# Forget-gate products of the next head queued in equal shares behind the score levels, and merge-gate blocks spread over three heads

## The chip, the cores and the metric

The kernel runs on one core of a Trainium2 chip. The metric is the device time of one execution in microseconds (us), the median of several runs. In the rows, PE is the matrix engine (TensorE) and PEld its weight loads, DVE is VectorE, ACT is ScalarE, POOL is GpSimd, and SP issues the DMA transfers.

## The reference, cut to what matters

One encoder layer over 1024 positions and 1024 channels. A combined projection of the normalised input gives, among others, `q`, two forget gates (forward and backward), the values, and two merge gates. The part around the change is the bidirectional gated recurrence with eight heads of 128 channels, and the sigmoid of one merge gate:

```python
f = lb + (1.0 - lb) * sigmoid(zf)          # forget gate, per direction
k = (1.0 - lb) * sigmoid(-zf)
S_t = diag(f_t) S_{t-1} + k_t v_t^T        # per head, forward and backward
o_t = S_t^T q_t
merged = sigmoid(ga) * (A @ W_a) + sigmoid(gb) * (Bm @ W_b)
```

After it come an output projection, a gated feed-forward block and a per-layer embedding gate, which the change doesn't touch.

## The kernel before, in words

Everything is float32. Large products are done as three passes of a reduced type (high by high, high by low, low by high): `mm3` at line 127 issues, for each of eight blocks of 128 input channels, three products with 512 moving columns into one PSUM bank, so 24 products for a block of 128 output channels and 512 positions (all recorded at L133).

The kernel goes through stages: input norm and token-major projections, the other branch, the channel-major columns (lines 514 to 548), **the heads** (lines 551 to 774), merge, output projection, feed-forward and the last gate. The change lies in the stage of the heads alone.

For each head `h` the loop at line 759 does, in program order:

- `scores(h)` (line 601). VectorE builds `ks` (L607) and `QA` (L606) from the head's `q`, keys `X`, `Y` and forget gates `F`. TensorE makes the diagonal score products (L613), then seven levels (block sizes 1 to 64). A level has two halves `g` of four score products (L624; each float32 product is two instructions of 128 columns). Between levels VectorE multiplies `QA` (L633) and `X` (L636) by forget gates, ScalarE copies a part of `Y` (L657), GpSimd makes the next `Y` (L660), VectorE merges scores under a mask (L646; ScalarE at the two last levels, L643), and `F` is folded to half its length (L666). The next level reads the updated `QA` and `X`.
- `proj(nxt, h + 1, "qfbg")` (line 561): the forget gates of the next head, in both directions. Two weight blocks are loaded and split (L114 and L115 behind the load in `load_split`), and for each of two halves of the positions `mm3` runs: 4 x 24 = 96 products. ScalarE and VectorE then write `F`, `X` and `Y` of that head (L591 to L599). `F` has one buffer, so the next head's is written only after the first level of the current head has read the old one; the `mm` tag of PSUM has three banks.
- `outputs(h, cur)` (line 670): 14 transposes of the last `X` and `Y` (L683), copied by ScalarE (L685), 28 instructions of state products (L688), a chain of state updates on VectorE (L692, L694), 44 instructions of output products (L712), a norm (L715, L719) and a last transpose (L722, L724).

At the last head, which has no next head to project, `gate_a(0)` and `gate_a(1)` (lines 766 and 769) compute four blocks of the merge gate (`j` from 4 to 7) for one half of the positions each: 8 x 24 = 192 products, and each call loads and splits the four weight blocks anew. The four earlier blocks of this gate are made in the stage before. `hT` is freed after these products, and the two halves `A0` and `A1` of the attention output are loaded and split into its place for `merge` (line 785).

The order of the instructions on each engine isn't the program's: the framework schedules at compile time, on a simulated timeline; among the instructions whose inputs and buffers are ready it takes the one that comes first in the program. On the chip each engine keeps that order. Products of `proj` and `gate_a` are thus put wherever TensorE has, by that timeline, nothing earlier in the program that is ready, limited by free PSUM banks and by `F`.

Of the kernel before, what the change touches and what calls it, by code (L numbers as in the profile page):

```python
# [17 lines left out]
P = 128  # L18
# [3 lines left out]
KD = D // P  # L22
# [13 lines left out]
def kernel(ctx: ExitStack, tc: tile.TileContext, a: dict, out: bass.AP):  # L36
# [7 lines left out]
    nc = tc.nc  # L44
# [72 lines left out]
    def load_split(src, shape, eng, pool, rpool, tag="whl"):  # L117

        raw = rpool.tile([P] + shape, F32, name="raw", tag="raw")
        nc.sync.dma_start(raw, src)  # L120
        hl = pool.tile([P, 2] + shape, F32R, name="whl", tag=tag)
        split_into(hl[:, 0], hl[:, 1], raw, eng)
        return hl
# [3 lines left out]
    def mm3(ps, lhs, rhs, nk):  # L127

        n = nk * len(PASSES)
        i = 0  # L130
        for k in range(nk):
            for lp, rp in PASSES:
                nc.tensor.matmul(ps, lhsT=lhs(lp, k), rhs=rhs(rp, k), start=(i == 0), stop=(i == n - 1))  # L133
                i += 1
# [6 lines left out]
    def fm_rhs(fm):  # L141
        return lambda p, k: fm[p][k // 4][:, k % 4, :]
# [29 lines left out]
    class Seven:  # L172


        def __init__(self, w, raw, t, ev, zbanks):
            self.w, self.raw, self.t, self.ev, self.zbanks, self.n = w, raw, t, ev, zbanks, 0
            self.first, self.second = None, None
# [113 lines left out]
    c_raw, rawp = phase("raw", 2)  # L291
# [259 lines left out]
    c_hg, hg = phase("hg")  # L551
    c_t, t1 = phase("s1t", 2)

    class Head:
        pass

    def view(t, off, dims):
        tv = t[:]
        return bass.AP(tv.tensor, tv.offset + off, [list(tv.ap[0])] + dims)

    def proj(s, h, kinds):

        for kind in kinds:
            if kind == "q":
                s.q = hg.tile([P, T], F32, name="q", bufs=2)
                nc.sync.dma_start(s.q, q_d[h])  # L570
                continue
            if kind == "g":
                s.zg = hg.tile([P, T], F32, name="zg", bufs=2)
                nc.sync.dma_start(s.zg, zg_d[h])
                s.v = hg.tile([P, NT, P], F32, name="v", bufs=2)
                nc.sync.dma_start(s.v, v_d[h])
                continue
            if kind == "f":
                s.F = hg.tile([P, 2, T], F32, name="F")
                s.X = hg.tile([P, T], F32, name="X0", bufs=2)  # L580
                s.Y = hg.tile([P, T], F32, name="Y", bufs=2)
            w = load_split(a["w_fm"][{"f": 8, "b": 16}[kind] + h], [KD, P], None, whlp, rawp)
            for n in range(2):
                ns = slice(n * NH, (n + 1) * NH)
                ps = ps_tile("mm")
                mm3(ps, lambda p, k: w[:, p, k, :], fm_rhs(hT[n]), KD)
                d = 0 if kind == "f" else 1
                om = oml[:, d, h:h + 1]
                Fd = s.F[:, 1 - d, ns]
                sg = t2(t1, "sk")  # L590
                nc.scalar.activation(sg, ps, AF.Sigmoid, scale=-1.0)  # L591
                nc.scalar.activation(Fd, ps, AF.Sigmoid)
                sv = sg.rearrange("p (t h) -> p t h", h=2)
                for par in range(2):
                    dst = (s.X if par == d else s.Y).rearrange("p (t h) -> p t h", h=2)
                    nc.scalar.activation(dst[:, n * NH // 2:(n + 1) * NH // 2, par], sv[:, :, par],
                                         AF.Identity, scale=om)
                nc.scalar.activation(Fd, Fd, AF.Identity, scale=om, bias=lbt[:, d, h:h + 1])
                nc.vector.tensor_scalar(out=Fd, in0=Fd, scalar1=TINY, scalar2=None, op0=ALU.max)  # L599

    def scores(h, s):
        q, X, Y, F = s.q, s.X, s.Y, s.F
        QA = hg.tile([P, 2, T], F32, name="QA", bufs=2)
        ks = hg.tile([P, T], F32, name="ks")
        SC = hg.tile([P, NT, P], F32, name="SC", bufs=2)
        nc.vector.tensor_tensor(out=QA, in0=view(q, 0, [[0, 2], [1, T]]), in1=F, op=ALU.mult)  # L606
        nc.vector.tensor_tensor(out=ks, in0=X, in1=Y, op=ALU.add)  # L607

        for g in range(2):
            sp = ps_tile("sc")  # L610
            for i in range(4):
                cs = slice((4 * g + i) * P, (4 * g + i + 1) * P)
                nc.tensor.matmul(sp[:, i * P:(i + 1) * P], lhsT=ks[:, cs], rhs=q[:, cs], start=True, stop=True)  # L613
            nc.scalar.activation(SC[:, 4 * g:4 * g + 4], sp.rearrange("p (c t) -> p c t", c=4), AF.Copy)

        for li, m in enumerate(LEVELS):
            nb = T // m
            cb = P // (2 * m)

            def level(g):  # L620
                sp = ps_tile("sc")
                for i in range(4):
                    c = 4 * g + i
                    nc.tensor.matmul(  # L624
                        sp[:, i * P:(i + 1) * P], lhsT=X[:, c * P:(c + 1) * P],
                        rhs=view(QA, c * P, [[2 * m, cb], [T + m, 2], [1, m]]), start=True, stop=True)
                return sp

            def update(g, X2):

                o, of = g * NH, g * nb // 2
                qd = [[T + m, 2], [2 * m, nb // 4], [1, m]]
                nc.vector.tensor_tensor(out=view(QA, o, qd), in0=view(QA, o, qd),  # L633
                                        in1=view(F, of + 1, [[nb - 1, 2], [2, nb // 4], [0, m]]), op=ALU.mult)
                dims = [[4 * m, nb // 8], [3 * m, 2], [1, m]]
                nc.vector.tensor_tensor(out=view(X2, o, dims), in0=view(X, o, dims),  # L636
                                        in1=view(F, nb + of + 1, [[4, nb // 8], [1 - nb, 2], [0, m]]), op=ALU.mult)

            def merge(g, sp):
                if m >= 32:  # L640
                    for p0 in range(0, P, m):
                        c0 = p0 ^ m
                        nc.scalar.activation(SC[p0:p0 + m, 4 * g:4 * g + 4, c0:c0 + m],  # L643
                                             sp.rearrange("p (c t) -> p c t", c=4)[p0:p0 + m, :, c0:c0 + m], AF.Copy)
                    return
                nc.vector.copy_predicated(  # L646
                    SC[:, 4 * g:4 * g + 4], masks[:, li, None, :].broadcast_to([P, 4, P]),
                    sp.rearrange("p (c t) -> p c t", c=4))

            X2 = hg.tile([P, T], F32, name="X", bufs=3)  # L650
            sp0 = level(0)
            update(0, X2)
            merge(0, sp0)
            sp1 = level(1)

            mid = [[4 * m, nb // 4], [1, 2 * m]]
            nc.scalar.activation(view(X2, m, mid), view(Y, m, mid), AF.Copy)  # L657
            update(1, X2)
            mid = [[4 * m, nb // 4], [m, 2], [1, m]]
            nc.gpsimd.tensor_tensor(out=view(Y, m, mid), in0=view(X, m, mid),  # L660
                                    in1=view(F, 0, [[4, nb // 4], [nb + 3, 2], [0, m]]), op=ALU.mult)
            X = X2
            merge(1, sp1)
            F2 = hg.tile([P, 2, nb // 2], F32, name=f"F{2 * m}", bufs=2 if m == 64 else 1)
            Fv = F.rearrange("p d (b h) -> p d b h", h=2)
            nc.vector.tensor_tensor(out=F2, in0=Fv[:, :, :, 0], in1=Fv[:, :, :, 1], op=ALU.mult)  # L666
            F = F2
        s.QA, s.SC, s.X, s.Y, s.F = QA, SC, X, Y, F
# [76 lines left out]
        split_into(w[:, 0], w[:, 1], raw)  # L745
        return w

    def gate_a(n):
        for j in range(NGA, KD):
            w = load_split(a["w_fm"][24 + j], [KD, P], None, whlp, rawp)  # L750
            ps = ps_tile("mm")
            mm3(ps, lambda p, k: w[:, p, k, :], fm_rhs(hT[n]), KD)
            sg = t2(t1, "sk")
            nc.scalar.activation(sg, ps, AF.Sigmoid)
            nc.sync.dma_start(sig_d[j, :, n * NH:(n + 1) * NH], sg)

    cur = Head()
    proj(cur, 0, "qfbg")
    for h in range(H):
        nxt = Head()  # L760
        scores(h, cur)
        if h + 1 < H:
            proj(nxt, h + 1, "qfbg")
        if h == H - 1:

            gate_a(0)
            A0 = new_fm("A0")
            load_A(0, A0, range(H - 1), 5)
            gate_a(1)
            A1 = new_fm("A1")  # L770
            wa = [split_wa(load_wa(j)) for j in range(2)]
        outputs(h, cur)
        cur = nxt
# [320 lines left out]
```

## Time and profile before

| | |
|---|---|
| three runs | 1965.67, 1969.12, 1968.33 us, median 1968.33 us |
| the profiled execution | 1966.99 us, with a span of 1965.2 us from the first to the last instruction |
| TensorE | 97% of the span busy, granted clock 0.997 on average |
| VectorE, ScalarE, GpSimd | 57%, 39%, 11% |
| the heads | from 564 us to about 1020 us of the span |

A row of the timeline gives the start, the length, the engine, the line, the operation and, in brackets, the idle time before it and what ended it. The length of a group of products includes a modelled end of the last one, so the distance between starts says how long TensorE was taken. A row of the windows gives for each engine the busy time in that stretch, then the granted clock of TensorE and the DMA share.

### The profile page before, as it was taken

Reading aid. Unit: us, or ns where it says so; the run is one execution under the profiler, and the core shown is the slowest. Engines: PE = TensorE matmul, PEld = TensorE weight load, DVE = VectorE, ACT = ScalarE, POOL = GpSimd, SP = SyncE. Lnnn points to the kernel's source line nnn. Section 1 sums busy time; section 2 is a strip of 40 time slices with the busy share of each in tenths; the row PEclk is TensorE's granted clock in tenths of the full one; section 3 lists DMA queues with packets and bytes.
Section 4 is the critical chain, followed back from the end, with each engine's and each line's share of the span. In section 5 each row is a group of like instructions: output and inputs, shape, how many; then the busy total and the mean of one; then the engine's idle time right before and its main releaser. Section 6 shows DMA issues by size and latency. Waiting matters only on the chain.

```text
span 1965.2 us, 24005 instructions
## 1 busy us (share of the span) xinstructions
PE 1910.8 (97%) x9264; PEld 1596.0 (81%) x9264; DVE 1120.0 (57%) x1712; ACT 757.2 (39%) x1424; POOL 206.7 (11%) x153
## 2 busy tenths in 40 slices
PE   7999999999999999999989998999999999999999
PEld 6887888888887888888877887888888888888887
DVE  7402385544348777777665468855554537545743
ACT  6312254343354545545441356433333324112321
POOL 2600000000012222222112100000000000001000
PEclk9999999999999999999999999999999999999999
DMA  7220245323231221212336333232222106315222
GB/s 292 93 88 27 87 172 170 130 105 110 86 123 33 70 71 63 66 55 68 126 106 208 107 99 103 97 112 78 89 76 86 65 33 209 108 65 163 92 102 79
DMA packets 82690, 201.86 MB, mean 103 GB/s; under 512 B 8720, under 2 KB 18064, under 8 KB 82576
## 3 DMA queue, kind: packets, MB, share of 16 engines
q1 hardware_dynamic: 82576, 200.33, 30.2%
q8 instruction: 73, 1.20, 0.3%
q14 instruction: 41, 0.34, 0.0%
HBM read 147.35 MB, written 52.95 MB: 102 GB/s over the span
## 4 chain that ended last, share of the span: by engine, by line
PE 90%; DVE 4%; ACT 2%; DMA 2%; POOL 1%; issue 1%; SPq 0%; DVEq 0%; POOLq 0%; ACTq 0%
PE ps_mm L133 29%; PE ps_mm L278 20%; PE ps_sc L133 11%; PE ps_sc L278 10%; PE ps_st L133 6%; PE ps_sc L624 4%; PE ps_o L278 2%; PE ps_o L712 2%; PE ps_tr L278 2%; PE ps_st L278 1%; DVE QA L633 1%; POOL Y L660 1%; PE ps_st L688 1%; ACT SC L643 0%; DMA raw<-in_w_gate_dram 0%
## 5 line engine op out<-in xcount | busy, mean ns | idle before, releaser
L278 PE MATMUL ps_mm<-T,w 128*128 128x512 f32 x1296 | 309.6, 389 | 0.0
L278 PEld LDWEIGHTS ps_mm<-T,w 128*128 128x128 f32 x1296 | 243.2, 188 | 50.7 <-ACT u L228 0.2
L115 DVE TENSOR_TENSOR whl<-raw,whl 128x1024 fp32r<-128x1024 f32 (+1 forms) x70 | 89.6, 1282 | 142.7 <-ACT whl L114 142.6
L660 POOL TENSOR_TENSOR Y<-X,F 128x512 f32<-128x512 f32 x56 | 92.4, 1651 | 696.1 <-DVE F L599 392.4
L624 PE MATMUL ps_sc<-QA,X 128*128 128x128 f32 x896 | 126.4, 288 | 16.9 <-DVE QA L633 16.9
L115 DVE TENSOR_TENSOR w<-sums,w 128x1024 fp32r<-128x1024 f32 x72 | 88.0, 1223 | 94.2 <-ACT w L114 94.2
L624 PEld LDWEIGHTS ps_sc<-QA,X 128*128 128x128 f32 x896 | 116.1, 192 | 26.1 <-DVE QA L633 19.0
L133 PE MATMUL ps_mm<-whl,act 128*128 128x512 f32 x528 | 134.1, 389 | 0.0
L114 ACT ACTIVATE whl<-raw 128x1024 fp32r<-128x1024 f32 (+1 forms) x78 | 79.1, 1017 | 120.2 <-PE ps_sc L133 52.4
L633 DVE TENSOR_TENSOR QA<-QA,F 128x512 f32<-128x512 f32 x112 | 91.8, 828 | 49.2 <-PE ps_sc L624 48.1
L133 PE MATMUL ps_mm<-hTb,whl 128*128 128x512 f32 x480 | 118.6, 396 | 0.0
L133 PEld LDWEIGHTS ps_mm<-whl,act 128*128 128x128 f32 x528 | 99.1, 188 | 20.7
L133 PE MATMUL ps_mm<-hTa,whl 128*128 128x512 f32 x480 | 115.1, 392 | 0.0
L114 ACT ACTIVATE w<-sums 128x1024 fp32r<-128x1024 f32 x72 | 75.9, 1055 | 99.9 <-PE ps_sc L278 76.9
L278 PE MATMUL ps_sc<-T,w 128*128 128x512 f32 x432 | 107.5, 389 | 0.0
L133 PEld LDWEIGHTS ps_mm<-hTa,whl 128*128 128x128 f32 x480 | 89.4, 188 | 18.1
L133 PEld LDWEIGHTS ps_mm<-hTb,whl 128*128 128x128 f32 x480 | 88.2, 188 | 16.8
L278 PEld LDWEIGHTS ps_sc<-T,w 128*128 128x128 f32 x432 | 81.1, 188 | 16.9
L133 PE MATMUL ps_sc<-whl,act 128*128 128x512 f32 x354 | 91.0, 390 | 0.3 <-ACT acc L953 0.3
L133 PEld LDWEIGHTS ps_sc<-whl,act 128*128 128x128 f32 x354 | 66.3, 188 | 14.3 <-ACT acc L953 0.7
L115 POOL TENSOR_TENSOR wpg<-raw,wpg 128x1024 fp32r<-128x1024 f32 x4 | 9.6, 2403 | 598.3 <-ACT wpg L114 593.6
L278 PE MATMUL ps_mm<-B,wA 128*128 128x512 f32 x264 | 67.3, 399 | 1.7 <-ACT wA L114 1.7
(309 smaller groups left out, 3574.2 us busy)
## 6 DMA issues: line engine op xcount, KB each, us to landing
raw<-in_w_fm_dram SPq DMA_DIRECT2D x52, 512.0 KB, 3.6
raw<-in_w_gate_dram SPq DMA_DIRECT2D x22, 512.0 KB, 3.4
raw<-in_w_up_dram SPq DMA_DIRECT2D x22, 512.0 KB, 3.9
act_d<-s SPq DMA_DIRECT2D x22, 512.0 KB, 2.8
raw<-in_w_down_dram SPq DMA_DIRECT2D x22, 512.0 KB, 4.4
raw<-act_d SPq DMA_DIRECT2D x22, 512.0 KB, 4.2
raw<-in_w_tm_dram SPq DMA_DIRECT2D x16, 512.0 KB, 4.1
pr_d<-vs SPq DMA_DIRECT2D x16, 256.0 KB, 5.9
```

The costliest lines, as they stand in the source:

```text
L114: nc.scalar.activation(hi, src, AF.Copy)
L115: (eng or nc.vector).tensor_tensor(out=lo, in0=src, in1=hi.bitcast(F32), op=ALU.subtract)
L133: nc.tensor.matmul(ps, lhsT=lhs(lp, k), rhs=rhs(rp, k), start=(i == 0), stop=(i == n - 1))
L278: nc.tensor.matmul(ps, lhsT=lhs(lp, k), rhs=rhs(rp, k), start=(first and i == 0), stop=(i == n - 1), skip_group_check=True)
L624: nc.tensor.matmul(sp[:, i * P:(i + 1) * P], lhsT=X[:, c * P:(c + 1) * P], rhs=view(QA, c * P, [[2 * m, cb], [T + m, 2], [1, m]]), start=T ...
L633: nc.vector.tensor_tensor(out=view(QA, o, qd), in0=view(QA, o, qd), in1=view(F, of + 1, [[nb - 1, 2], [2, nb // 4], [0, m]]), op=ALU.mult)
L660: nc.gpsimd.tensor_tensor(out=view(Y, m, mid), in0=view(X, m, mid), in1=view(F, 0, [[4, nb // 4], [nb + 3, 2], [0, m]]), op=ALU.mult)
L688: nc.tensor.matmul(up[:, i * P:(i + 1) * P], lhsT=kt[:, i], rhs=v[:, c], start=True, stop=True)
L712: nc.tensor.matmul(op[:, i * P:(i + 1) * P], lhsT=l, rhs=r, start=(j == 0), stop=(j == len(terms) - 1))
```

## The change

A small class `Pace` replaces `mm3` for the products of `proj` (from head 1 on) and of `gate_a`. Each product is traced under `tc.issue_after(mark)`, which adds an order edge on TensorE's own queue: the product is put behind the marked instruction, and doesn't wait for it to finish. The marks of a head are eight: the last diagonal score product, and the last score product of the second half of each of the seven levels. The products are dealt out in equal shares: product `i` of `n` goes behind mark `i * 8 // n`, so 12 of 96 behind each mark, or 18 of 144 at the heads 4 and 6, where one block of the merge gate (48 products for both halves) follows the next head's forget gates. At the last head the two remaining blocks make 96. The blocks 4 and 5 of the gate load their weights once for both halves, the blocks 6 and 7 still twice: six loads and splits in place of eight.

```diff
+    class Pace:
+        def __init__(self, marks, n):
+            self.marks, self.n, self.i = marks, n, 0
+
+        def mm3(self, ps, lhs, rhs, nk):
+            n = nk * len(PASSES)
+            i = 0
+            for k in range(nk):
+                for lp, rp in PASSES:
+                    with tc.issue_after(self.next()):
+                        nc.tensor.matmul(ps, lhsT=lhs(lp, k), rhs=rhs(rp, k), start=(i == 0), stop=(i == n - 1))
+                    i += 1
+
+        def next(self):
+            mark = self.marks[min(self.i * len(self.marks) // self.n, len(self.marks) - 1)]
+            self.i += 1
+            return mark
...
-                mm3(ps, lambda p, k: w[:, p, k, :], fm_rhs(hT[n]), KD)
+                (pace.mm3 if pace else mm3)(ps, lambda p, k: w[:, p, k, :], fm_rhs(hT[n]), KD)
...
-                nc.tensor.matmul(sp[:, i * P:(i + 1) * P], lhsT=ks[:, cs], rhs=q[:, cs], start=True, stop=True)
+                mark = nc.tensor.matmul(sp[:, i * P:(i + 1) * P], lhsT=ks[:, cs], rhs=q[:, cs], start=True, stop=True)
...
+        s.marks = [mark.ins]
...
-                    nc.tensor.matmul(
+                    mark = nc.tensor.matmul(
...
+                if g == 1:
+                    s.marks.append(mark.ins)
...
-    def gate_a(n):
-        for j in range(NGA, KD):
-            w = load_split(a["w_fm"][24 + j], [KD, P], None, whlp, rawp)
+    def gate_a(j, ns):
+        w = load_split(a["w_fm"][24 + j], [KD, P], None, whlp, rawp)
+        for n in ns:
             ps = ps_tile("mm")
-            mm3(ps, lambda p, k: w[:, p, k, :], fm_rhs(hT[n]), KD)
+            pace.mm3(ps, lambda p, k: w[:, p, k, :], fm_rhs(hT[n]), KD)
...
+    pace = None
     cur = Head()
     proj(cur, 0, "qfbg")
     for h in range(H):
         nxt = Head()
         scores(h, cur)
+        pace = Pace(cur.marks, 144 if h in (4, 6) else 96)
         if h + 1 < H:
             proj(nxt, h + 1, "qfbg")
+        if h in (4, 6):
+            gate_a(NGA + h // 2 - 2, range(2))
         if h == H - 1:
 
-            gate_a(0)
+            for j in (6, 7):
+                gate_a(j, [0])
             A0 = new_fm("A0")
             load_A(0, A0, range(H - 1), 5)
-            gate_a(1)
+            for j in (6, 7):
+                gate_a(j, [1])
             A1 = new_fm("A1")
```

## Rows read from the trace of the kernel before

**Rows 1.** The page, part 1: TensorE's busy time, share of the span, instructions.

```profile
PE 1910.8 (97%) x9264; PEld 1596.0 (81%) x9264; DVE 1120.0 (57%) x1712; ACT 757.2 (39%) x1424; POOL 206.7 (11%) x153
```

**Rows 2.** The windows of the heads' stage, one head or part of it each.

```profile
745.70:798.55 52.85, 49.01 (x320) 43.95 (x319) 40.53 (x71) 27.59 (x71) 14.02 (x9) 1.00 0.20 66
...
904.25:957.10 52.85, 52.85 (x334) 47.30 (x332) 43.06 (x67) 28.35 (x69) 11.28 (x8) 1.00 0.36 120
957.10:1010.00 52.90, 49.63 (x317) 43.71 (x315) 32.03 (x59) 19.27 (x54) 8.22 (x7) 1.00 0.30 96
1010.00:1030.00 20.00, 16.07 (x87) 13.22 (x87) 8.84 (x19) 9.06 (x33) 2.01 (x2) 0.91 0.29 96
```

**Rows 3.** TensorE's waits from 565 to 1050 us: total, times, longest.

```profile
PE ps_sc L624 <- DVE QA L633: 16.9, 25, 1.5
PE ps_tr L683 <- ACT kt L685: 6.5, 5, 1.3
PE ps_tr L722 <- ACT on L719: 2.9, 1, 2.9
```

**Rows 4.** TensorE's timeline of one head's period, its thinly filled part and its fillers.

```profile
732.69 0.33 PE L683 MATMUL ps_tr<-ident,X 128*128 128x128 f32 x1 [1.28 <-ACT kt L685]
...
733.97 1.49 PE L624 MATMUL ps_sc<-QA,X 128*128 128x128 f32 x8
...
736.25 1.59 PE L624 MATMUL ps_sc<-QA,X 128*128 128x128 f32 x8 [0.46 <-DVE QA L633]
737.66 0.84 PE L688 MATMUL ps_st<-v,kt 128*128 128x128 f32 x6
739.52 1.23 PE L624 MATMUL ps_sc<-QA,X 128*128 128x128 f32 x8 [1.02 <-DVE QA L633]
740.49 5.26 PE L133 MATMUL ps_mm<-hTb,whl 128*128 128x512 f32 x22
745.60 0.65 PE L624 MATMUL ps_sc<-QA,X 128*128 128x128 f32 x4
...
772.76 1.95 PE L624 MATMUL ps_sc<-QA,X 128*128 128x128 f32 x16
...
775.81 2.05 PE L624 MATMUL ps_sc<-QA,X 128*128 128x128 f32 x16 [0.67 <-DVE QA L633]
```

**Rows 5.** TensorE's timeline where the stage of the heads starts.

```profile
558.86 5.60 PE L133 MATMUL ps_mm<-hTb,whl 128*128 128x512 f32 x24
564.30 5.60 PE L133 MATMUL ps_mm<-hTa,whl 128*128 128x512 f32 x24
569.74 3.79 PE L133 MATMUL ps_mm<-hTb,whl 128*128 128x512 f32 x16
573.36 1.95 PE L613 MATMUL ps_sc<-q,ks 128*128 128x128 f32 x16
575.07 2.07 PE L133 MATMUL ps_mm<-hTb,whl 128*128 128x512 f32 x8
```

**Rows 6.** ScalarE's and VectorE's timelines there: from the last product to the first scores.

```profile
564.50 0.60 ACT L591 ACTIVATE sk<-ps_mm 128x512 f32<-128x512 f32 x1 [2.84 <-PE ps_mm L133]
...
565.47 1.06 ACT L114 ACTIVATE whl<-raw 128x1024 fp32r<-128x1024 f32 x1
...
567.70 1.22 DVE L607 TENSOR_TENSOR ks<-X,Y 128x1024 f32<-128x1024 f32 x1
```

**Rows 7.** TensorE's timeline at the end of the stage, and the window behind it.

```profile
979.37 5.49 PE L133 MATMUL ps_mm<-A,whl 128*128 128x512 f32 x23
...
1017.86 1.10 PE L722 MATMUL ps_tr<-ident,on 128*128 128x128 f32 x4 [2.92 <-ACT on L719]
1019.90 1.09 PE L722 MATMUL ps_tr<-ident,on 128*128 128x128 f32 x4 [0.94 <-DVE on L724]
...
1020.00:1024.00 4.00, 3.93 (x13) 2.83 (x13) 3.39 (x6) 2.52 (x6) 0.00 (x0) 0.63 0.11 27
```

## The prediction, on record before the changed kernel ran

> **What bounds the kernel now.** I read the page first: TensorE is busy for 97% of the span [rows 1], so time can come only from its idle stretches or from work that it no longer does, and the change removes no product. Then the windows of the stage it touches [rows 2]. A head in the middle of the loop takes 52.85 us and TensorE is busy for 49.01 of them, 3.84 idle, five times nearly alike; VectorE has 40.53 and ScalarE 27.59, so neither is the bound, but VectorE is near enough to matter as a chain. From 904 to 957 us, where the merge-gate products lie beside head 6, TensorE is busy without a gap; after that 3.27 and 3.93 us are idle.
>
> Next, who TensorE waits for [rows 3]: 16.9 us for VectorE's update of `QA` between levels, in 25 waits of at most 1.5 us, 6.5 us for ScalarE's copies of the state transposes, 2.9 us once for the last norm. The three come to 26.3 us, 1.3% of the run: hardly more can be won from labelled waits.
>
> The timeline says where in a head they lie [rows 4]. The fillers, products of a coming head, are all used between level 1 and level 4: 22 of them start at 740.49, after the second wait of the levels, and the run of fillers is over by 772.76. Level 4, level 5, the next head's first scores and its level 0 stand there with little else, and the waits are there. So the forget-gate products are enough in number (96 per head, at (564.30 - 558.86) / 24 = 0.227 us each 21.8 us [rows 5]) and lie in the wrong place. The code gives the reason: three banks take the products of a head one ahead, and they stop when these are full.
>
> **The change part by part.** The sum is made against the profiled execution, 1966.99 us (span 1965.2 and 1.8 around it); the median of the three runs, 1968.33, is 1.3 above it.
>
> *(a) Filler behind every level.* A share of 12 is 2.72 us, more than the longest wait for `QA`, 1.5 us [rows 3]. A wait behind a marked half is thus covered. Not covered is a wait between the two halves of a level, since only the second half carries a mark: level 0 waits 0.46 us there now [rows 4], with transposes and state products beside it. I leave 0.46 in each of seven heads, 3.2, and remove 16.9 - 3.2: **-13.7**. Bounds: all 16.9 goes; or four levels of each head keep 0.46 (the three others run both halves in one go, as at 772.76 and 775.81 [rows 4]), 12.9, and 4.0 goes.
>
> *(b) Ends of products that nothing covers.* Sixteen score instructions take 575.07 - 573.36 = 1.71 us of the queue [rows 5], 0.107 each. The eight at 736.25 need 0.86, but the next work starts 1.41 later, at 737.66, and the sixteen at 775.81 show 2.05 instead of 1.71 [rows 4]: 0.55 + 0.34, about 0.9 us per head that counts as busy and isn't. Six heads: **-5.4**, between 0 and -5.4. [...]
>
> *(c) The start.* The 24 + 16 products of head 1 that fill 564.30 to 573.36 before head 0's first scores [rows 5] go behind those scores. TensorE then has nothing until `ks` is made, 567.70 + 1.22 = 568.92 [rows 6]: a new gap of 4.6 us, while the scores come 4.4 earlier than now. **+4.6**; nothing in the program can fill it.
>
> *(d) The seam between heads.* This is the price of the change. The last 12 products of the next head are queued behind the last level, so its keys are made just in time: from the last product to `ks` the same chain runs (two sigmoids and two scalings on ScalarE, L607 on VectorE), 4.6 us with the weight split of 1.06 in it [rows 6], about 3.6 without; I take 4.1. Waiting behind it are the scores of the next head, and with them its levels; its own first share is queued behind them too. What covers it is `outputs` of the head just finished. Of its 14 transposes and 28 state products (42 instructions of 0.107 us, 4.5 us) I count two thirds as ready then, 3.0 us, as they alternate with copies on a busy ScalarE; 1.1 us per head is left, seven seams: **+7.7**. Bounds: 0, where it is all covered, and 4.6 x 7 = 32.2, where nothing is. The nearest row is the wait for the copy of a transpose at the same place now, 1.28 us [rows 4], close to the lower end.
>
> *(e) Switching.* The 22 products that start at 740.49 would end at 745.48, and the next score starts at 745.60 [rows 4]: 0.12 lost by a change of product. Eight shares in place of four runs of filler, seven heads: 28 x 0.12 = **+3.4**, between 0 and twice that.
>
> *(f) The end.* Merge products that need only the first seven heads already serve as filler, 23 of them at 979.37 [rows 7]. With `A0` made during head 7 they come later, and can lie beside the last head's outputs, where TensorE waits 2.92 and 0.94 us [rows 7]: **-3.9**, or 0 where they don't.
>
> *Costed at nothing.* Two weight loads and splits fewer (one is 1.06 on ScalarE [rows 6]): the engine has idle time in the same stretch [rows 2], so nothing on the path goes. The gate's 192 products are the same number at another place; the 48 more in heads 4 and 6 make shares of 18, 4.1 us, which lie behind the marks as the others do. In exchange head 6 loses its gapless stretch [rows 2], which (d) counts with seven seams. The second half `A1` is loaded after the last share of head 7 rather than well before; its cover is the last head's outputs, whose last transpose stands at 1019.90 [rows 7]. Were that gone, seven splits of half the size of the 1.06 us one would stand on the path, about 4 us.
>
> Sum: -13.7 - 5.4 + 4.6 + 7.7 + 3.4 - 3.9 = **-7.3**, 1959.7 for the profiled execution, **1961.0** beside the median.
>
> **The rivals.**
>
> *The seam decides, and it is slower.* If the transposes wait for `X` and `Y`, or their copies for ScalarE behind the evacuation of the last block, (d) is 4.6 per head, 32.2 in all: -7.3 + 24.5 = +17.2, 1985.5. For it speaks that all of the next head hangs on its last 12 products, where now they run a head ahead. Against it speaks that the outputs have 4.5 us of products. It ends slower than before once the seam costs more than 2.1 us per head (7.7 + 7.3 = 15.0, over seven), slower by 0.2% from 2.7.
>
> *The waits only move.* All levels of block size under 16 wait between their halves once the fillers no longer lie there: (a) keeps 12.9, not 3.2. That is +9.7, so +2.4: 1970.7, no change. For it speaks that the 22 fillers of 740.49 stand just between the halves of level 1 [rows 4], which no mark asks for. Against: outputs of the head before are taken first when ready, and have 94 small pieces (14 + 28 + 44 + 8), 10 us of them.
>
> *More than forecast.* The seam is covered whole, and the waits for copies, 6.5 [rows 3], go with it, since fillers are left everywhere: -7.3 - 7.7 - 6.5 = -21.5, 1946.8. For it: VectorE's chain is 40.5 of 52.85 us [rows 2], so TensorE always has something left to do by the end of a head.
>
> [...]
>
> *It doesn't do what it says.* The edges only forbid an earlier place. Where the scheduler has more urgent work the shares pile up behind the last level and the fillers lie in one run again, only later; that ends in the first rival.
>
> **How the numbers follow.** A measurement of this kernel tells about 0.2%, 4 us, from no change. Chances: the forecast 0.37; slower by the seam 0.24; waits that only move 0.20; more than forecast 0.14; the clock 0.05. The forecast lies 7.3 under the time before, so it counts as faster but for a little: faster 0.37 + 0.14, slower 0.24 and some of the clock's, 0.28, the rest the same, 0.21. The forecast alone reaches from 1951 to 1969, by halving or doubling (d) and by (a), (b) and (f) at half. The range of 8 in 10 takes in the case of more gain with a little under it, and most of the slower case, which spreads from 1972 to 1999: 1944 to 1982.
>
> **What would show it.** Right: in the timeline of a middle head, runs of 12 forget-gate products behind each level, the total of waits for `QA` under 6 us, the distance between the first scores of two heads under 52 us. A gap of 4 to 5 us before the first scores of head 0 shows (c). Wrong: a wait of TensorE for `ks` (L607) of more than 2 us at every head, the same 17 us for `QA` under the second or third halves, or clock under 1.00 in the windows of the seams.

## The result: slower by 1.65%, and the profile after

Before 1968.22 us (median of four runs, 1965.67 to 1969.12), after **2000.77 us** (1997.73 to 2001.64): ratio 1.0165, interval 1.0147 to 1.0182. Forecast were 1961.0 with 1944 to 1982 as the range: the sign is wrong, and the result lies outside the range.

In the rows of after, line numbers are 21 to 24 higher: L634 are the diagonal scores (L613), L646 the scores of the levels (L624), L657 the update of `QA` (L633), L660 that of `X` (L636), L690 the fold of `F` (L666), L627 and L628 the making of `QA` and `ks`, L709 the copy of the transposes (L685), L712 the state products (L688), L718 the state updates (L694), L743 the last norm (L719), L746 the last transpose (L722). L612 to L620 write `F`, `X` and `Y` from a finished block of forget-gate products (L591 to L599); this is called its evacuation below. The paced products have a line of their own, L567. A **seam** is the place where one head's outputs meet the next head's first scores.

First the page. The same 9264 instructions of TensorE as in [rows 1], 18 us more of busy time, and 34.3 us more of span (1999.5 against 1965.2), so the loss is only half idle time:

```profile
PE 1929.0 (96%) x9264; PEld 1612.0 (81%) x9264; DVE 1116.6 (56%) x1710; ACT 756.1 (38%) x1422; POOL 209.0 (10%) x153
```

The window of the heads' stage, of before (from 558.86 us on, where [rows 5] begin) and of after, between the same instructions:

```profile
558.86:1023.16 464.30, 432.36 (x2713) 384.16 (x2712) 343.17 (x583) 233.52 (x585) 109.84 (x72) 1.00 0.21 68
```

```profile
562.29:1058.59 496.30, 447.49 (x2714) 397.75 (x2712) 342.50 (x581) 232.05 (x583) 112.83 (x72) 0.95 0.19 62
```

This answers where the time went: 32.0 of the 34.3 us are here. Idle time of TensorE is 48.8 instead of 31.9, **16.9 more**. Busy time is 447.5 instead of 432.4, **15.1 more for the same products**, at a granted clock of 0.95 instead of 1.00. The rest is 3.4 us that fell ahead of the stage and 1.1 gained behind it, where the change touches nothing.

By stretches: the stage's start is 4.4 shorter (10.1 us to the first scores, 14.5 before), the seven heads up to the last one's first scores take 400.3 instead of 376.6, and the last head to the end of the stage takes 85.9 instead of 73.2. Three kinds of work moved between these stretches: 40 products of head 1 left the start (9.1 us), 23 gate products, 5.2 us, came to the last head (96 there, 73 before), and 16 small instructions of the outputs, 1.7 us, moved there from head 6. With that taken off, the start lost 4.7, the heads 21.5 and the last head 5.8.

The windows of single heads after, from first scores to first scores. A middle head took 52.85 us in [rows 2]:

```profile
626.52:684.14 57.62, 51.44 (x319) 46.16 (x319) 41.79 (x72) 27.66 (x71) 13.58 (x10) 0.94 0.18 60
...
739.32:798.29 58.97, 50.97 (x321) 45.87 (x319) 42.56 (x72) 27.57 (x71) 15.12 (x10) 0.92 0.20 63
...
860.28:912.94 52.66, 49.31 (x320) 44.56 (x319) 34.34 (x66) 27.31 (x71) 10.71 (x8) 0.98 0.23 78
912.94:972.66 59.72, 59.03 (x352) 51.76 (x351) 48.40 (x82) 28.57 (x73) 16.80 (x11) 0.99 0.13 42
```

Heads 1 and 3 (the first two rows) are 5 to 6 us longer, with 6 to 8 us idle and a clock of 0.92 to 0.94. Head 5, which follows a head with gate products, is as long as before, 52.66. That difference is the clue to what follows.

TensorE's waits in the stage; [rows 3] had `QA` 16.9 in 25 and `kt` 6.5 in 5, and the kernel before waited for `S` once, 1.6 us:

```profile
PE ps_st L712 <- ACT kt L709: 17.0, 6, 3.9
PE ps_st L712 <- DVE S L718: 11.0, 3, 5.3
PE ps_sc L646 <- DVE QA L657: 10.7, 5, 4.1
PE ps_sc L634 <- DVE ks L628: 4.5, 1, 4.5
```

Twenty-five short waits became a few long ones. Where they lie is seen in TensorE's timeline, here around the seam between heads 2 and 3, with head 0's first scores ahead of it and one row each of the next seam and of the one at 860 behind it:

```profile
572.40 3.79 PE L634 MATMUL ps_sc<-q,ks 128*128 128x128 f32 x16 [4.51 <-DVE ks L628]
...
730.85 3.02 PE L567 MATMUL ps_mm<-hTb,whl 128*128 128x512 f32 x12
...
737.99 1.16 PE L712 MATMUL ps_st<-v,kt 128*128 128x128 f32 x8 [2.58 <-ACT kt L709]
...
739.32 1.95 PE L634 MATMUL ps_sc<-q,ks 128*128 128x128 f32 x16
...
744.21 1.57 PE L646 MATMUL ps_sc<-QA,X 128*128 128x128 f32 x8
751.07 1.65 PE L712 MATMUL ps_st<-v,kt 128*128 128x128 f32 x6 [5.30 <-DVE S L718]
...
795.78 2.07 PE L712 MATMUL ps_st<-v,kt 128*128 128x128 f32 x8 [2.58 <-ACT kt L709]
...
868.32 1.59 PE L646 MATMUL ps_sc<-QA,X 128*128 128x128 f32 x8 [0.46 <-DVE QA L657]
```

There are two kinds of hole. The first, for the copy of the transposes, is 2.57 to 2.77 us at five seams, 13.1 in all. The second lies inside level 0 of a new head, behind its first half: 4.06, 3.49, 2.78, 5.30 and 2.20 us in heads 0 to 4, 17.8 in all. In heads 0 and 2 it ends with the first update of `QA`. In heads 1, 3 and 4 state products of the head in front stand first in TensorE's queue and wait for `S`, whose updates lie behind the same work on VectorE.

What fills the first hole is on ScalarE. Its timeline there:

```profile
733.90 0.60 ACT L612 ACTIVATE sk<-ps_mm 128x512 f32<-128x512 f32 x1 [2.00 <-PE ps_mm L567]
734.39 0.59 ACT L613 ACTIVATE F<-ps_mm 128x512 f32<-128x512 f32 x1
734.87 1.06 ACT L114 ACTIVATE whl<-raw 128x1024 fp32r<-128x1024 f32 x1
...
736.65 0.81 ACT L619 ACTIVATE F<-F,lbt,oml 128x512 f32<-128x512 f32 x1
737.35 0.59 ACT L709 ACTIVATE kt<-ps_tr 128x512 f32<-128x512 f32 x1
```

The copy that the state products want stands behind the whole evacuation of the last projection block and a weight split. The second hole is on VectorE; its timeline, with one `ks` of a later head:

```profile
737.38 1.22 DVE L628 TENSOR_TENSOR ks<-X,Y 128x1024 f32<-128x1024 f32 x1
...
738.97 2.29 DVE L627 TENSOR_TENSOR QA<-q,F 128x2048 f32<-128x2048 f32 x1
741.18 2.84 DVE L660 TENSOR_TENSOR X<-X,F 128x256 f32<-128x256 f32 x2
743.93 1.22 DVE L690 TENSOR_TENSOR F<-F 128x1024 f32<-128x1024 f32 x1
...
745.28 2.05 DVE L660 TENSOR_TENSOR X<-X,F 128x256 f32<-128x256 f32 x2
...
748.12 1.84 DVE L660 TENSOR_TENSOR X<-X,F 128x256 f32<-128x256 f32 x2
...
751.08 0.68 DVE L657 TENSOR_TENSOR QA<-QA,F 128x512 f32<-128x512 f32 x1
...
847.16 1.22 DVE L628 TENSOR_TENSOR ks<-X,Y 128x1024 f32<-128x1024 f32 x1
```

After `ks` come 2.29 us for `QA`, then the `X` updates and folds of three levels, and only at 751.08 the first update of `QA`; TensorE has stood still since 745.8. All but the small updates of `S` is work on the new head's own `F` and `X`.

The same instruction in the kernel before, VectorE's timeline, and the scores that it serves, TensorE's:

```profile
698.45 1.21 DVE L607 TENSOR_TENSOR ks<-X,Y 128x1024 f32<-128x1024 f32 x1
```

```profile
729.46 1.95 PE L613 MATMUL ps_sc<-q,ks 128*128 128x128 f32 x16
```

Call the time from the end of `ks` to the first scores the **lead** of a head. Before it is 729.46 - 699.66 = 29.8 us: the chain of a head runs while the head in front of it is under way. After it is 739.32 - 738.60 = 0.7, and 1.2 to 1.9 at the four other seams with a hole for `kt`. At the heads from 860.28 and 972.66 it is 860.28 - 848.38 = 11.9 and 13.4: there 48 gate products fill the last marks, the forget gates end some two levels earlier, and both holes are absent (0.46 at 868.32). Head 6, with a lead of 1.2, has the first hole and not the second. Its shares are 18 products and not 12, but so are those of head 4, where the hole is 2.20; in head 6 the first update of `QA` also comes sooner, 9.5 us behind the first scores instead of 10.5 in head 4 and 11.8 in head 3. Which of the two decides, no run separates.

Around the second hole the granted clock is lower. Windows of it and of what follows it:

```profile
746.00:751.00 5.00, 0.00 (x0) 0.00 (x0) 5.00 (x10) 0.63 (x1) 2.33 (x2) 0.65 0.00 0
751.00:754.00 3.00, 2.93 (x13) 2.93 (x14) 2.20 (x8) 0.00 (x0) 0.00 (x0) 0.50 0.02 5
754.00:758.00 4.00, 4.00 (x24) 3.49 (x23) 1.56 (x3) 0.77 (x2) 0.00 (x0) 0.96 0.00 0
```

TensorE is back at work from 751 on, at a granted clock of 0.50, and from 754 on at 0.96. The eight state products at 795.78 take 2.07 us behind a hole of 2.58, at 0.50 (window 795.78 to 797.85); the eight at 737.99, behind a hole as long, take 1.16 at 1.00 (window 737.99 to 739.15).

### The profile page after: what moved, and what is told of

It is laid out like the page before. It is cut to its first block, busy times and chain, and to the rows that moved or that the text cites. A ratio compares the mean times of both kernels' runs of the same rounds, so it can differ in the third digit from the quotient of the medians.

```text
span 1999.5 us, 24040 instructions
## 1 busy us (share of the span) xinstructions
PE 1929.0 (96%) x9264; PEld 1612.0 (81%) x9264; DVE 1116.6 (56%) x1710; ACT 756.1 (38%) x1422; POOL 209.0 (10%) x153
## 4 chain that ended last, share of the span: by engine, by line
PE 90%; DVE 6%; ACT 2%; DMA 1%; issue 1%; POOL 0%; SPq 0%; DVEq 0%; POOLq 0%; ACTq 0%
PE ps_mm L278 20%; PE ps_mm L133 19%; PE ps_sc L133 11%; PE ps_sc L278 10%; PE ps_mm L567 9%; PE ps_st L133 6%; PE ps_sc L646 5%; DVE X L660 2%; PE ps_tr L278 2%; PE ps_o L278 2%; PE ps_o L736 2%; PE ps_st L278 1%; DVE QA L627 1%; PE ps_st L712 1%; DVE F L690 1%
## 5 line engine op out<-in xcount | busy, mean ns | idle before, releaser
L646 PE MATMUL ps_sc<-QA,X 128*128 128x128 f32 x896 | 125.7, 290 | 11.4 <-DVE QA L657 10.7
L646 PEld LDWEIGHTS ps_sc<-QA,X 128*128 128x128 f32 x896 | 118.0, 197 | 18.4 <-issue 7.8
L657 DVE TENSOR_TENSOR QA<-QA,F 128x512 f32<-128x512 f32 x112 | 81.2, 725 | 65.4 <-PE ps_sc L646 65.1
L567 PE MATMUL ps_mm<-hTa,whl 128*128 128x512 f32 x432 | 113.9, 410 | 0.0
L567 PE MATMUL ps_mm<-hTb,whl 128*128 128x512 f32 x432 | 112.7, 404 | 0.0
L278 PEld LDWEIGHTS ps_sc<-T,w 128*128 128x128 f32 x432 | 81.1, 188 | 16.9
L567 PEld LDWEIGHTS ps_mm<-hTa,whl 128*128 128x128 f32 x432 | 81.8, 196 | 15.8
L567 PEld LDWEIGHTS ps_mm<-hTb,whl 128*128 128x128 f32 x432 | 78.8, 190 | 14.7
L660 DVE TENSOR_TENSOR X<-X,F 128x256 f32<-128x256 f32 x112 | 76.8, 722 | 0.2
```

The costliest lines, as they stand in the source:

```text
L646: mark = nc.tensor.matmul(sp[:, i * P:(i + 1) * P], lhsT=X[:, c * P:(c + 1) * P], rhs=view(QA, c * P, [[2 * m, cb], [T + m, 2], [1, m]]), ...
```

## The experiments

All of them compute the whole reference. The short diffs are against the changed kernel, unless the text says otherwise. Each was run in three rounds beside the kernel before, whose median was 1968.6 to 1969.8 in these batches.

**Which part loses.** The gate blocks spread and paced as in the change, the forget gates left as they were (`Pace` over 48 products in heads 4 and 6):

```diff
-                (pace.mm3 if pace else mm3)(ps, ...)
+                mm3(ps, ...)
```

> Only the merge-gate blocks are paced and spread over heads 4, 6 and 7; the forget-gate products go where the scheduler puts them, as before. Theory A (the loss is that the next head's forget gates are held back to the end of a head, so that its keys, QA, X and folds on ScalarE and VectorE can no longer be made ahead): 1962 to 1972 us, with the five middle heads again near 52.9 us. Theory B (the loss comes from the gate blocks: longer shares at heads 4 and 6, and a thin last head): 1990 or more.

Measured 1973.20, ratio 1.0024 (1.0013 to 1.0035), 1.2 above theory A's range: a cost of 4 us, not the loss. The reverse, forget gates in shares, and the gate of before:

```diff
-        if h in (4, 6):
-            gate_a(NGA + h // 2 - 2, range(2))
...
-            for j in (6, 7):
-                gate_a(j, [0])
+            gate_a(0)
```

> Only the forget-gate products are paced; the merge-gate blocks are all at the last head again, unpaced, as before. Theory A: 1995 to 2005 us, and the wait for the copies of the state transposes and the stretch of low clock at each seam as in the changed kernel. Theory B: 1965 to 1975.

Measured 2010.31, ratio 1.0213 (1.0198 to 1.0228), 5 above theory A's range and far from B's. The shares of the forget gates carry all of the loss and 10 us more; the gate blocks in heads 4 and 6 give those 10 back. Its waits:

```profile
PE ps_st L712 <- DVE S L718: 15.9, 4, 5.3
PE ps_st L712 <- ACT kt L709: 15.5, 6, 2.6
PE ps_sc L646 <- DVE QA L657: 9.9, 5, 4.5
```

`S` waits 4.9 longer than in the change itself. The parts don't add up, and the leads of 11.9 and 13.4 say why: in the change the gate blocks stand in for a lead at two seams. Without them the lead of head 5 is 1.6 and it has both holes, 2.58 and 2.74.

**Fewer marks.** If only the last shares hurt, then dealing the same products over the first six, three or one of the marks should help, as the last product comes earlier:

```diff
-        pace = Pace(cur.marks, 144 if h in (4, 6) else 96)
+        pace = Pace(cur.marks[:6], 144 if h in (4, 6) else 96)
```

> The changed kernel with the shares behind the first six marks only (16 products each, 24 at heads 4 and 6), so that the next head's gates are done two levels before the end of a head. Theory A: the seam gets shorter, 1975 to 1990 us. Theory C (the loss is not at the seam but between the halves of the levels, where shares behind second halves give no cover): the same 2000 or more, since two levels now have no share at all.

> The changed kernel with the shares behind the first three marks only (32 products each, 48 at heads 4 and 6): the next head's gates are done by the middle of a head. Theory A: most of the loss is gone, 1965 to 1982 us, waits for QA at the late levels come back. Theory C: 2000 or more.

> The changed kernel with all products behind the first mark alone: no shares, each head's forget-gate products only may not start before the diagonal scores of the head in front of it. Theory A2 (what costs is the lead that is lost: before, three of the four blocks of a head were computed during the head two in front and lay ready in the banks): still 1990 to 2005 us. Theory D (the shares behind the levels cost, by their order): 1964 to 1975 us.

Measured: six marks 1998.45, ratio 1.0153 (1.0136 to 1.0170); three 1996.96, 1.0146 (1.0131 to 1.0162); one, which leaves no shares at all, 2009.17, 1.0218 (1.0191 to 1.0245). The lead does come back (from head 1 on it is 7.5 to 25.6 us with three marks and 4.8 to 23.9 with one), but the time doesn't. With six marks hardly a wait for `kt` is left (0.7), and others are there instead. The largest of them, and what VectorE does ahead of one of its five cases, at 793.72:

```profile
PE ps_sc L646 <- DVE ov L99: 12.4, 5, 2.5
```

```profile
791.28 2.29 DVE L627 TENSOR_TENSOR QA<-q,F 128x2048 f32<-128x2048 f32 x1 [1.70 <-PE ps_o L736]
```

The label is the norm of the last outputs (L99), an instruction of 0.16 us. What takes the time is in front of it, the making of the head's own `QA`, of which there are two buffers: it starts when the output products (L736) of the head two in front, which still read the buffer that it takes, are through. VectorE waits 8.5 us for them at five heads. So `ks` was early there and `QA` was not. The last two levels, now without a share, wait for ScalarE's merges, 6.3, and the first scores behind them 6.2. The waits with one mark:

```profile
PE ps_sc L646 <- DVE QA L657: 27.4, 13, 5.5
PE ps_tr L746 <- ACT on L743: 12.0, 3, 5.4
```

Now the late levels starve, worse than before the change (16.9). So an early end of the products is not enough: 96 products of the one next head covered the late levels or were done early, in none of these kernels both. That each step only traded one wait for another was not expected; theory A's ranges failed at six and three marks, and one mark came out 4 above A2's. Theory C, a loss between the halves of the levels, came nearest by its number (2000 or more), but its waits aren't there: beyond the first level the changed kernel waits 3.9 us for `QA`, and the fastest kernel below has its shares behind second halves too.

**The lead kept, and shares as well.** The kernel before solved this by stock: three of the four blocks of a head were multiplied a head ahead and waited in the three banks (those of the head that scores at 729.46 are through at 667.05, and ScalarE copies their `F` out of the banks from 686.64 on, L592). Here those 72 products go in shares of 12 behind levels 1 to 6 of the head two in front, the fourth block is free, and the gate is as before:

```diff
-        pace = Pace(cur.marks, 144 if h in (4, 6) else 96)
+        pace = Pace(prev.marks[2:], 72) if prev else None
...
-        cur = nxt
+        prev, cur = cur, nxt
```

> From the kernel before: the first three blocks (72 products) of a head go in shares of 12 behind levels 1 to 6 of the head two in front of it, the fourth is free; the merge-gate blocks stay at the last head. The lead is kept and the late levels get filler. Theory A2: no loss, 1950 to 1968 us, waits for QA under 10 us. Theory D: 1985 or more.

Measured 1973.21, ratio 1.0025 (1.0015 to 1.0034), 5 above A2's range. The loss is gone but for 4 us, and early heads are shorter than before (675.39 to 722.28, 46.9 us). Three later ones, with leads of 18.4, 9.6 and 9.6, wait 2.5 us ahead of level 0 as with six marks, for a `QA` that is made when the output products are through. One mark more, so that the 72 reach behind the diagonal scores of the head in front:

```diff
-        pace = Pace(prev.marks[2:], 72) if prev else None
+        pace = Pace(prev.marks[2:] + cur.marks[:1], 72) if prev else None
```

> As the run with shares and lead, with a seventh mark, the next head's diagonal scores: shares of 10 to 11, so that the seam has filler too. Theory A2: 1948 to 1968 us, a little under the six marks. Theory D: 1985 or more.

Measured **1949.51**, ratio 0.9904 (0.9889 to 0.9919): faster than both kernels. Two heads in the windows, the wait for `QA`, and the lead of one head, first on VectorE, then on TensorE:

```profile
625.18:674.35 49.17, 47.23 (x309) 42.31 (x308) 39.07 (x69) 27.32 (x71) 11.16 (x10) 1.00 0.13 46
674.35:724.07 49.72, 48.83 (x321) 43.62 (x320) 40.65 (x75) 27.67 (x72) 14.59 (x10) 1.00 0.24 84
```

```profile
PE ps_sc L646 <- DVE QA L657: 8.0, 14, 2.1
```

```profile
700.77 1.21 DVE L628 TENSOR_TENSOR ks<-X,Y 128x1024 f32<-128x1024 f32 x1
```

```profile
724.07 1.95 PE L634 MATMUL ps_sc<-q,ks 128*128 128x128 f32 x16
```

A lead of 724.07 - 701.98 = 22.1 us, clock 1.00, 0.9 to 1.9 us idle per head against 3.84 in [rows 2], half the waits for `QA`. This is what the change was forecast to do, with the one thing that it took away put back. Against the kernel with shares for the forget gates alone, 2010.31, it differs in that and in the last 24 products of a head, which are free; the free block by itself was not tried.

**VectorE's order at the seam.** The second hole is `X` work that stands ahead of the first update of `QA`. Here the `X` updates of a level are issued behind the last update of `QA` of the level before:

```diff
+                qa = nc.vector.tensor_tensor(out=view(QA, o, qd), ...)
...
-                nc.vector.tensor_tensor(out=view(X2, o, dims), ...)
+                with tc.issue_after(s.qa) if li else ExitStack():
+                    nc.vector.tensor_tensor(out=view(X2, o, dims), ...)
```

On the changed kernel, and on the one before as a control:

> The changed kernel with an order on VectorE: the update of X of a level is queued behind the QA update of the level before it, so that at the seam the QA update of the first level no longer stands behind the X work of the two levels after it (5 us of VectorE in the third head). Theory E (that queue on VectorE is the main loss at the seam): 1980 to 1992 us. Theory A2: 1995 to 2008, since the work itself is still all there between two heads.

> The kernel before with the same order on VectorE (X of a level behind the QA update of the level before). Theory E (the queue in front of the QA update is a matter of the seam, which only the changed kernel has): no gain here, 1964 to 1985 us, since X work lies where VectorE has time. If the order is simply a better one for any kernel: 1950 or less, as the 22 us that it gave the changed kernel.

Measured 1978.84, ratio 1.0052 (1.0035 to 1.0068), 1 below theory E's range and 16 below A2's, and 1953.87, 0.9926 (0.9912 to 0.9941), between the two ranges. The first alone would have passed for proof that the queue on VectorE was two thirds of the loss. The control says otherwise: the order is worth 15.2 us without the change too. Between the two kernels 25.0 of the 32.6 us remain, so about 8 belong to this order. What is left in the changed kernel (its line numbers are 3 higher from the copies on):

```profile
PE ps_st L715 <- ACT kt L712: 13.9, 6, 2.9
PE ps_sc L646 <- DVE QA L657: 7.0, 7, 3.0
...
PE ps_st L715 <- DVE S L721: 4.0, 4, 1.9
```

The second hole shrank (`S` from 11.0 to 4.0, `QA` from 10.7 to 7.0); the first, behind ScalarE's evacuation, stayed. The same order on three other kernels: on the one with the lead, and on those with one and with six marks.

> The shares with lead and seven marks, plus the order on VectorE. With the lead kept there is no seam for the order to mend: 1945 to 1958 us, the same within 0.4%. Rival (the order gains by itself): 1940 or less.

> One mark, no shares, no lead, plus the order on VectorE. Without shares it was 2009 us. If the lost lead shows mainly as that queue on VectorE, the order gains here too: 1985 to 1995 us. If the late levels without filler are what costs here, the order doesn't help: 2003 to 2012.

> Shares behind the first six marks plus the order on VectorE. Theory F (with the queue on VectorE gone, what is left at the seam is ScalarE's evacuation of the last block and the copies behind it, 2.6 us at six heads, and keys that are ready earlier take it away): 1965 to 1976 us, under the 1978.8 of eight marks. If an earlier end of the shares only starves the last levels: 1979 or more.

Measured 1950.54, ratio 0.9904 (0.9887 to 0.9920); 2010.52, 1.0215 (1.0200 to 1.0230); 1993.65, 1.0130 (1.0115 to 1.0145). With the lead the order gives nothing more: both cut the waits for `QA`, to 8.0 (lead), 8.3 (order, in the kernel before) and 9.0 (both), and 1950 is what they come to together. Without shares it gives nothing either. With six marks it gives perhaps 5 us (the two intervals overlap), and not the drop that the theory of ScalarE's copies foretold: moving the evacuation earlier frees the copies, but the wait for a `QA` made late (12.4, as with six marks above) and those for ScalarE's merges (5.7 and 4.9) take their place.

**Is the low clock a cost of its own?** Ten products that serve nothing per seam, written into the bank of the first state products ahead of them, and in a second kernel twenty more in level 0; they should keep TensorE busy through the holes:

```diff
+    def filler(ps, mark, n):
+        for i in range(n):
+            with tc.issue_after(mark):
+                nc.tensor.matmul(ps, lhsT=hT[0][0][0][:, 0, 0:P], rhs=hT[0][0][0][:, 0, :], start=True, stop=True)
...
                 up = ps_tile("sc" if h == H - 1 and d else "st")
+                if g0 == 0 and d == 0 and h < H - 1:
+                    filler(up, tr.ins, 10)
...
                 sp = ps_tile("sc")
+                if li == 0 and g == 1 and h > 0:
+                    filler(sp, s.half, 20)
```

> The changed kernel with ten extra products (128x512, 0.227 us each at full clock) per seam, written into the bank of the first state products ahead of them and overwritten by them, so that TensorE works on through most of its 2.6 us wait for the copy of the transposes; nothing else changes, and the program has 70 products more (15.9 us of work). Theory G (the lower clock after a hole is a cost of its own, which goes when the hole is filled with anything): the granted clock rises from 0.984 and the time falls although there is more work, to 1986 to 1994. Rival H (the holes themselves are the whole loss, the clock falls in stretches where TensorE has slack anyway): no gain, 2000 to 2005.

> As the ten extra products, and twenty more per seam into the bank of level 0's second half ahead of its scores, where TensorE waits some 5 us for VectorE: 210 products more (47.7 us of work at full clock), all in holes as the trace of the changed kernel shows them. Theory G: clock 0.99 or more, labelled waits at the seams nearly gone, and 1978 to 1988, since of the 21 us that the lower clock cost about 15 come back. Rival H: 2000 to 2010, the extra products take the place of the waits and, where a hole is shorter than they are, lengthen it.

> The kernel with the update of QA ahead of X's on VectorE (1978.8) and the ten extra products per seam. Its waits for the copies were 13.9 us in six places of about 2.6, with sixteen scores of 3.5 us in place of 1.7 behind them. Theory G: 1966 to 1972, the scores back at 1.7 to 2.1 us. Rival H: 1978 to 1983.

Measured 2004.37, ratio 1.0180 (1.0163 to 1.0197); 2005.21, 1.0181 (1.0166 to 1.0196); 1993.05, 1.0118 (1.0103 to 1.0133). The third is the kernel with the `X` updates issued later, 1978.84, with the ten products. No kernel gained, and the third lost 14 us: theory G's times failed in all three, H's came in the first two, and the third is 10 above H's. The third's waits show why (line numbers 5 to 10 higher):

```profile
PE ps_tr L756 <- ACT on L753: 8.4, 3, 2.9
PE ps_sc L651 <- DVE QA L662: 8.1, 6, 3.0
PE ps_st L722 <- DVE S L728: 5.9, 6, 1.9
...
PE ps_st L722 <- ACT kt L717: 3.0, 5, 0.7
```

The wait for `kt` is nearly gone, but the listed waits sum to 35.8 against 34.4 without the fillers: other waits took its place, and 15.9 us of added products came on top, almost in full. The window of the whole stage in the second kernel, between the same instructions as in the first windows above:

```profile
560.63:1063.39 502.76, 480.05 (x2924) 425.56 (x2922) 342.57 (x582) 233.08 (x583) 117.93 (x72) 0.98 0.19 61
```

This row tells G from H. The 21 us in the expectation are an estimate: in the changed kernel's windows of 1 us, the busy time times what the granted clock lacks of 1.00 sums to 21.4 over the stage. Idle time is 22.7 instead of 48.8. Busy time without the 210 added products (47.7 us at 0.227 each, an estimate) is 432.4, where the changed kernel has 447.5 and the kernel before 432.4. So with the holes filled and the clock at 0.98 the 15.1 us of slower work are gone: G's mechanism, a cost of its own, is what the busy time shows, though its times failed, for 47.7 us of useless work bought 26.1 and 15.1.

## Why the prediction was wrong, step by step

**(d), the seam, is the step that failed.** It reckoned a chain from the last product to `ks`, 4.1 us with 3.0 covered, 1.1 left at each of seven seams, 7.7. The chain to `ks` was nearly right: 733.9 to 738.6 is 4.7, with the whole weight split of 1.06 in it, of which the step took half. Two things were wrong. The cover, `outputs`, was counted as ready; its state products need a copy by ScalarE that stands behind the evacuation, so the cover is behind the same chain, and 2.6 us stay uncovered. And the chain doesn't end at `ks`: `QA`, the first `X` updates and folds are as new, 13.7 us of VectorE from the start of `ks` to the first update of `QA` at 751.08. The waits are 13.1 for `kt` and 13.8 in level 0 of heads 1 to 4, **26.9** at the seams where 7.7 were forecast. That is towards the upper bound, 32.2, which the step had written down and set aside because the nearest row was a wait of 1.28; that row came from a kernel with a lead of 29.8 us. With 26.9 in its place the sum is +11.9, about 1980: slower, but still inside the range.

**The first rival** described this: copies "for ScalarE behind the evacuation of the last block". It gave 1985.5. What it lacked is **the clock**, which has a chance of its own, 0.05, and no term in the sum. A stretch like that of [rows 7], 4 us at 0.63, loses 4 x (1 - 0.63) = 1.5 us, 10.4 at seven seams, as an estimate. The two were made exclusive, with chances of 0.24 and 0.05, though holes and a lower clock came together here, 0.50 behind the holes that end at 751.07 and 795.78. Added up, -7.3 + 24.5 + 10.4 = +27.6 for the profiled execution, against 34.3 measured. No run shows 1.5 us at each seam (behind the hole that ends at 737.99 the clock is 1.00); what the trace shows is 15.1 us more busy time for the same products, at 0.95 over the stage. With that the sum above leaves the range: 11.9 + 15.1 = +27.0, about 1995. Leaving the clock out was the second step that failed.

**(a), filler behind every level,** held beyond the first level. Of the waits for `QA`, 4.06 and 2.78 are the second hole of heads 0 and 2; the rest, 0.79, 0.46 and 2.65 in the last head, is 3.9 in place of 16.9: 13.0 gone, 13.7 forecast. There the shares do what they were said to do.

**(c), the start,** was 4.6; the wait for `ks` before head 0's first scores is 4.51, and the stretch lost 4.7. It left out the 4.06 of level 0 in head 0, which has the same cause as (d).

**(f), the end,** was -3.9. The last head's transposes wait as before, 2.92 and 0.94, with another 3.93 for `kt` that no term had, and the stretch lost 5.8 beyond the work moved there. ScalarE's rows for that wait:

```profile
1038.66 0.63 ACT L114 ACTIVATE A<-xr 128x512 fp32r<-128x512 f32 x1 [5.29 <-DMA xr<-at_d]
1039.20 0.58 ACT L709 ACTIVATE kt<-ps_tr 128x512 f32<-128x512 f32 x1
```

The copy stands behind a split of a half of `A`, which waits 5.29 us for its load. Merge products did not lie beside those waits: 48 of them were multiplied within the last head in both kernels.

**(b) and (e)** can't be read: busy time moved by 15.1 at a lower clock, which hides terms of 5.4 and 3.4. That (b) comes on top of the labelled waits was the author's estimate; no run shows it. In the kernel with the lead, 1949.51, the stage's busy time at a clock of 0.99 is 432.0 against 432.4, where the two forecast -2.0 together. **Costed at nothing:** fewer splits show no wait; the later `A` does, by the 3.93 above; the gate's place was not nothing, it was a gain of 10 where the forget gates are paced and a cost of 4 where they aren't.

The added idle time is thereby accounted for: 13.0 for `QA`, 6.5 for the copies of [rows 3], as the third rival had it, and 2.9 in two single waits, for a split of `A` and for `S`, are gone; 4.5, 4.1, 26.9 and 3.9 came. That is +17.0, with 16.9 measured.

Of the signs named, the runs of 12 behind each level came, and so did the wait at head 0. Waits for `QA` under 6 us and heads under 52 us did not (10.7 in all, and 52.7 to 62.0), and the clock under 1.00 at the seams did (0.50 from 751 to 754). A wait for `ks` of over 2 us at every head did not come: TensorE stands one step earlier, at `kt`, and one later, in level 0. Whoever had looked for `ks` alone would have found the seam free.

What is shown: the paced forget gates carry the loss (first two runs), a stock of 72 products with nearly the same shares takes it away (with leads of 22 to 29 us from head 1 on in the faster of the two runs), and within the changed kernel the two seams with leads of 11.9 and 13.4 us have neither hole. Of the 32.0 us in the stage 16.9 are idle time and 15.1 slower work; that the second goes when the holes are filled rests on one kernel and an estimate.

## What to carry to other kernels

Before work is tied to a later place, read how far ahead of its use it is done now: the time from the end of a stage's first product to the first reader is a stock, and the change spends it. At a seam, follow the chain on every engine until the work is again steady, not just to the first operand (with six marks `ks` was early and `QA` was not), and ask of each cover whether it stands in the same queue. Holes and a lower clock came together here, 16.9 us more idle time and 15.1 of slower work, so their prices had to be added.

## What was not expected of the hardware

Behind two holes of 2.58 us the granted clock was 0.50 once (795.78: eight products in 2.07 us) and 1.00 once (737.99: eight in 1.16). The clock's part was nearly as large as the holes' own: 15.1 us of slower work beside 16.9 us of added waiting, where the one stretch of [rows 7] comes to 1.5 us.
